# Two plain weight pairs instead of one at the head of each down unit, and the working pools moved to the other end of on-chip memory, in a two-layer decoder trunk on one core

## The chip, the core and the metric

The kernel runs on one core of a Trainium2 chip. The core has a matrix engine (TensorE, "PE" in the profile, with its weight loads as "PEld"), a vector engine (VectorE, "DVE"), a scalar engine (ScalarE, "ACT"), GpSimd ("POOL") and SyncE ("SP"), which issues the DMA transfers. Each engine works through its own list of instructions in order; the engines wait for each other through semaphores. Operands lie in the on-chip memory SBUF; matmul results are summed in PSUM, which has eight banks of 128 x 512 fp32 numbers. The metric is the time of one execution on the device in microseconds (us).

## What is computed

The reference is two layers over 256 tokens of width 2048, all in fp32. Each layer projects the normalised input, runs two groups of attention heads (gated linear attention and stick-breaking attention), projects their outputs back and adds them; then comes the part that the change touches:

```python
hm = rms_norm(x, mlp_norm)
up = jnp.square(jax.nn.relu(jnp.einsum('bsd,df->bsf', hm, w_up)))   # f = 8192
return x + jnp.einsum('bsf,fd->bsd', up, w_down)
```

## The kernel before

**How fp32 is multiplied.** Each fp32 operand is split into a high part in a format that the matrix engine takes whole, and a low part that is the rest. One product is then three matmuls: high by high, high by low, low by high. Weights are split when they arrive: ACT copies the raw tile to `whi`, DVE subtracts to get `wlo` (L358 and L360 in the other stages, `parts`, L987 to L992, in the down stage). There are four `whi` and four `wlo` buffers.

**Stages of the MLP.** The hidden width of 8192 is worked off in four quarters `q`. For each quarter, `mlp_up` computes eight pairs `i` of 256 hidden columns (L424 and L428 are its matmuls), applies the norm factor, the ReLU and the square, and splits the result into its parts (`up_forms`, L941). Then `mlp_down(q)` multiplies that quarter by its 2048 rows of `w_down`. With two layers there are eight such down stages.

**The down stage.** It has two units, `n2` = 0 and 1, of 1024 output columns each. A unit sums over eight pairs `j` of 128-row blocks. All its sums stay in eight PSUM banks, `m1` to `m8`, until the unit ends. There are two kinds of pair:

- A plain pair has two items, `left` (banks m2 and m4) and `right` (m3 and m8). Each item needs one `parts` call of 1024 elements per partition, and issues 12 matmuls.
- A fast pair multiplies 2 x 2 blocks with seven products instead of eight. It has four items with 6, 3, 6 and 6 matmuls; the third uses banks m5 and m7, the fourth m1 and m6. DVE first forms sums of weight blocks (L1042 to L1046), and `up_forms` has made sums of the activation blocks (tile `sx`, L945 to L952). `fast(i)` (L955) says which pairs are fast, for `up_forms` and for the down stage alike: 1, 3 and 5.

When the last fast pair of a unit has run (`lastf`, L1035), `drain` (L1049) adds banks 5, 1, 6 and 7 into the residual tiles `xb`: one ACT copy and eight DVE operations. After the `left` item of pair 7 `drain_left` adds banks 2 and 4 (two DVE operations), and after its `right` item `drain_right` adds banks 3 and 8. In the last stage each of these adds is followed by a store of the output (L1029). The next unit takes the same eight banks again, so its first matmul into a bank waits until that bank has been added.

**What sets the order.** Within the down stage the order on PE, DVE and ACT is written out by hand (`manual_schedule`, L1129). A list `queue` keeps items prepared ahead (`LEAD` = 4, L1098): item i+3 is prepared, then item i is multiplied, then whatever follows item i (a drain) is issued. So on DVE a drain stands behind the preparation of the item three places on, and everything that is prepared later stands behind the drain. At the edges of the stage a scheduler mixes the neighbouring stage's instructions in. The order is fixed when the program is built.

**Loads.** `load(x)` (L970) fetches pair x of the stage, 1 MB, four pairs ahead. Two of five go to buffers in the stage's own pool (`raw2`), three of five to buffers in the weight pool (`raw`).

**Where PSUM goes next.** After the down stage the eight banks become two accumulators of two banks (banks of m5, m1 and of m6, m7) and four single-bank tiles `ps`. After layer 0's last down stage the second layer begins with transposes of `xb` into `ps` tiles (`norm_operand`, L294); the first of these tiles has the bank of m2 and the second that of m8.

**Pools.** SBUF pools are stacked from the low end: constants, residual tiles, activations (`act`), weights (raw, whi, wlo), temporaries, small statistics, and on top the pool of the current stage, which is opened and closed by `open_scope` (attention tiles, or for the MLP `sx`, `ts`, `t4` and `raw2`).

Of the kernel before, what the change touches and what calls it, by code (L numbers as in the profile page):

```python
# [39 lines left out]
def trunk_kernel(  # L40
# [26 lines left out]
    cpool = ctx.enter_context(tc.tile_pool(name="const", bufs=1))  # L67
    xpool = ctx.enter_context(tc.tile_pool(name="resid", bufs=1))
    apool = ctx.enter_context(tc.tile_pool(name="acts", bufs=19))
    wpool = ctx.enter_context(tc.tile_pool(name="weights", bufs=3))  # L70
    tpool = ctx.enter_context(tc.tile_pool(name="temps", bufs=2))
    spool = ctx.enter_context(tc.tile_pool(name="stats", bufs=6))

    pools = {}
    scopes = {}
# [28 lines left out]
    def tmp(tag, shape, dt=F32, bufs=2):  # L104
        pool = pools["att"] if tag in ATT else pools["mlp"] if tag in MLP else tpool
        return pool.tile(list(shape), dt, tag=tag, name=nm(tag), bufs=bufs)
# [497 lines left out]
    for l in range(DEPTH):  # L604
# [336 lines left out]
        def up_forms(op, i, t):  # L941


            if fast(i):
                a11, a21, a12, a22 = (t[:, k, r * P : (r + 1) * P] for k in range(2) for r in range(2))  # L945
                e = tmp("t2", [P, 3, P], bufs=4)
                d = op.x[i] = tmp("sx", [P, 3, 2, P], F32R, bufs=3)
                nc.vector.tensor_tensor(e[:, 2, :], a21, a11, ALU.subtract)
                nc.vector.tensor_tensor(a21, a21, a22, ALU.subtract)
                nc.vector.tensor_tensor(e[:, 0, :], a11, a21, ALU.subtract)  # L950
                nc.vector.tensor_tensor(e[:, 1, :], a12, e[:, 0, :], ALU.subtract)
                split(d, e)  # L952
            split(op.pair(i), t)

        def fast(i):  # L955
            return i in (1, 3, 5)

        hT = Operand()
        ssq2 = new_ssq()
# [1 line left out]
        def mlp_down(q):  # L961
# [25 lines left out]
            def parts(r, n=2):  # L987
                hi = wpool.tile([P, 2, 512], F32R, tag="whi", name=nm("whi"), bufs=4)
                lo = wpool.tile([P, 2, 512], F32R, tag="wlo", name=nm("wlo"), bufs=4)
                nc.scalar.activation(hi[:, :n], r, AF.Copy)  # L990
                nc.vector.tensor_tensor(lo[:, :n], r, f32(hi[:, :n]), ALU.subtract)  # L991
                return hi, lo  # L992

            def mm(m, a, w, c, last):

                (ah, al), (wh, wl) = a, w
                o = banks[m]
                nc.tensor.matmul(o, ah, wh[:, c], start=m not in begun, stop=False)
                begun.add(m)
                nc.tensor.matmul(o, ah, wl[:, c], start=False, stop=False)  # L1000
                nc.tensor.matmul(o, al, wh[:, c], start=False, stop=last)

            def add(dst, a, b, sub=False):
                nc.vector.tensor_tensor(dst, a, b, ALU.subtract if sub else ALU.add)  # L1004
# [6 lines left out]
            def steps(x):  # L1011

                n2, j = pairs[x]
                last = j == 7
                r = raws[x]
                d = op.t[j]
                x11, x21, x12, x22 = (xb[2 * n2 + c][:, tt, :] for c in range(2) for tt in range(2))

                def blk(k, tt):
                    sl = slice(tt * P, (tt + 1) * P)  # L1020
                    return d[:, k, 0, sl], d[:, k, 1, sl]

                def ext(i):
                    return op.x[j][:, i, 0, :], op.x[j][:, i, 1, :]

                def store(c, tt):
                    if end:
                        n = 2 * n2 + c
                        nc.sync.dma_start(  # L1029
                            ov[:, tt, n * 512 : (n + 1) * 512], xb[n][:, tt, :]  # L1030
                        )

                if fast(j):
                    sums = {}
                    lastf = j == 5  # L1035

                    def first():
                        t13 = sums["t13"] = tmp("ts", [P, 2, 512], bufs=2)
                        t4 = sums["t4"] = tmp("t4", [P, 512], bufs=1)
                        b12 = r[:, 0, 512:]  # L1040
                        ends = r.rearrange("p k (c n) -> p (k c) n", c=2)[:, ::3, :]
                        nc.vector.tensor_tensor(  # L1042
                            t13, ends, b12.unsqueeze(1).to_broadcast([P, 2, 512]), ALU.add
                        )
                        add(b12, t13[:, 0, :], r[:, 1, 512:])
                        add(t4, b12, r[:, 1, :512])  # L1046
                        return parts(r[:, 1, :].rearrange("p (c n) -> p c n", c=2))

                    def drain():  # L1049
                        dw = tmp("t2", [P, 512], bufs=4)  # L1050
                        nc.scalar.activation(dw, banks[1], AF.Copy)
                        add(x12, banks[5], x12)
                        add(x22, banks[5], x22)
                        add(x11, banks[1], x11)
                        add(dw, banks[6], dw, True)
                        add(x12, dw, x12)
                        add(dw, banks[7], dw)
                        add(x21, x21, dw, True)
                        add(x22, dw, x22)

                    return (
                        (first, lambda w: (mm(2, blk(1, 0), w, 0, False), mm(3, ext(1), w, 1, False)), None),
                        (lambda: parts(sums["t4"].unsqueeze(1), 1), lambda w: mm(4, blk(1, 1), w, 0, False), None),
                        (lambda: parts(sums["t13"]),
                         lambda w: (mm(5, blk(0, 1), w, 0, lastf), mm(7, ext(2), w, 1, lastf)), None),
                        (lambda: parts(r[:, 0, :].rearrange("p (c n) -> p c n", c=2)),
                         lambda w: (mm(1, blk(0, 0), w, 0, lastf), mm(6, ext(0), w, 1, lastf)),
                         drain if lastf else None),
                    )

                def left(w):
                    for m, tt in ((2, 0), (4, 1)):
                        for k in range(2):
                            mm(m, blk(k, tt), w, k, last and k == 1)

                def right(w):
                    for m, tt in ((3, 0), (8, 1)):
                        for k in range(2):
                            mm(m, blk(k, tt), w, k, last and k == 1)

                def drain_left():
                    add(x11, banks[2], x11)
                    store(0, 0)
                    add(x21, banks[4], x21)
                    store(0, 1)

                def drain_right():
                    add(x12, banks[3], x12)
                    store(1, 0)
                    add(x22, banks[8], x22)  # L1090
                    store(1, 1)

                return (
                    (lambda: parts(r[:, :, :512]), left, drain_left if last else None),
                    (lambda: parts(r[:, :, 512:]), right, drain_right if last else None),
                )
# [13 lines left out]
            for x in range(len(pairs)):  # L1110
                load(x + 4)
                for prepare, products, follow in steps(x):
                    queue.append((x, products, prepare(), follow))
                    if len(queue) >= LEAD:
                        emit(*queue.pop(0))
# [25 lines left out]
def build(shapes):  # L1141
    import concourse.bacc as _bacc
    import numpy as _np
    from concourse import mybir as _mybir

    nc = _bacc.Bacc("TRN2", target_bir_lowering=False, num_devices=1)
    args = []
    for name in _INS:
        shape, dtype = shapes[name]
        args.append(  # L1150
            nc.dram_tensor(
                f"in_{name}_dram", shape, _mybir.dt.from_np(dtype), kind="ExternalInput"
            ).ap()
        )
    for i, (shape, dtype) in enumerate(_OUTS):
        dt = _mybir.dt.from_np(_np.dtype(dtype))
        args.append(nc.dram_tensor(f"out_{i}_dram", shape, dt, kind="ExternalOutput").ap())
    with tile.TileContext(nc) as tc:
        trunk_kernel(tc, *args)
    return nc  # L1160
# [10 lines left out]
```

## Time and profile before

| | |
|---|---|
| three runs | 2243.92, 2244.15, 2244.21 us, median 2244.15 us |
| profiled execution | 2244.34 us, its span 2242.6 us |
| granted TensorE clock | 1.000 over the span |
| PE busy | 2219.7 us, 99% of the span |
| DVE busy | 1628.6 us, 73% |
| ACT busy | 1171.0 us, 52% |
| DMA | 409.05 MB, mean 182 GB/s |

Times in the profile count from the start of the span. A row of the timeline gives the start, the duration, the engine, the source line, the operation, output tile `<-` input tiles, sizes and the number of merged instructions; in brackets stand the idle time before it and what ended that. Buffer numbers are left out of most tile names, but the banks show as `m__860` and the like: each unit numbers its banks anew, in the order m5, m1, m6, m7, m2, m4, m3, m8. Matmuls overlap in the pipeline: the next starts some 0.23 us after the one before, though each is shown with a duration near 0.39 us. So rates are read from starts. DVE operations too start up to 0.09 us before the one before has ended.

### The profile page before, as it was taken

How to read it: one execution, taken by the hardware profiler on the slowest of the kernel's cores; microseconds unless marked ns; L12 is line 12 of the kernel's file. 1: busy time of each engine (PE TensorE's matmuls, PEld its weight loads, DVE VectorE, ACT ScalarE, POOL GpSimd, SP SyncE). 2: the span in 40 equal slices, each digit the busy share in tenths (PEclk: the TensorE clock that was granted, in tenths of full speed). 3: DMA queues.
4: the chain of work that ended last, by engine and by line, in shares of the span. 5: the costliest groups of instructions: out<-in, count | busy, mean ns of one | idle time of the engine just before them, and what ended most of it. 6: DMA issues, size and time to landing. Idle time of an engine off the chain costs nothing.

```text
span 2242.6 us, 28461 instructions
## 1 busy us (share of the span) xinstructions
PE 2219.7 (99%) x11292; PEld 1858.6 (83%) x11292; DVE 1628.6 (73%) x2024; ACT 1171.0 (52%) x1499; POOL 39.1 (2%) x68
## 2 busy tenths in 40 slices
PE   9999999999999999999999999999999999999998
PEld 7988778887888888788788887888878878887887
DVE  5777565668868868867967775656787688688688
ACT  5555354555555455455555553555555545554553
POOL 0020000000000000000000200000000000000000
PEclk9999999999999999999999999999999999999999
DMA  6545446664665665565446544466656656656653
GB/s 228 189 158 162 151 144 232 187 188 169 214 186 188 201 188 187 190 195 179 169 135 204 171 151 150 154 225 184 188 183 203 187 178 207 188 181 210 185 180 127
DMA packets 250857, 409.05 MB, mean 182 GB/s; under 512 B 6650, under 2 KB 162882, under 8 KB 250724
## 3 DMA queue, kind: packets, MB, share of 16 engines
q1 hardware_dynamic: 250724, 407.24, 55.7%
q8 instruction: 88, 1.44, 0.3%
q14 instruction: 45, 0.37, 0.0%
HBM read 405.12 MB, written 2.10 MB: 182 GB/s over the span
## 4 chain that ended last, share of the span: by engine, by line
PE 91%; DVE 7%; issue 1%; ACT 1%; DMA 0%; POOL 0%; SPq 0%; POOLq 0%
PE acc L424 24%; PE acc L428 12%; PE acc L377 9%; PE acc L378 9%; PE acc L379 9%; DVE wlo L991 3%; DVE xb L1004 2%; DVE t L1004 1%; PE ps L294 1%; PE ps L847 1%; PE ps L859 1%; DVE ts L1042 0%; PE ps L806 0%; ACT whi L990 0%; PE ps L540 0%
## 5 line engine op out<-in xcount | busy, mean ns | idle before, releaser
L360 DVE TENSOR_TENSOR wlo<-raw,whi 128x1024 fp32r<-128x1024 f32 (+2 forms) x530 | 630.5, 1194 | 420.0 <-ACT whi L358 418.9
L358 ACT ACTIVATE whi<-raw 128x1024 fp32r<-128x1024 f32 (+2 forms) x530 | 545.3, 1032 | 643.9 <-PE acc L424 340.0
L424 PE MATMUL acc<-act,whi 128*128 128x512 f32 x2304 | 816.0, 399 | 0.0
L428 PE MATMUL acc<-act,wlo 128*128 128x256 f32 x2304 | 646.8, 281 | 0.0
L424 PEld LDWEIGHTS acc<-act,whi 128*128 128x128 f32 x2304 | 433.0, 188 | 106.5
L428 PEld LDWEIGHTS acc<-act,wlo 128*128 128x128 f32 x2304 | 435.2, 189 | 0.4
L377 PE MATMUL acc<-whi,act 128*128 128x512 f32 (+2 forms) x960 | 368.4, 384 | 0.5 <-ACT act L302 0.5
L378 PE MATMUL acc<-wlo,act 128*128 128x512 f32 (+2 forms) x960 | 361.9, 377 | 0.4 <-DVE wlo L360 0.4
L379 PE MATMUL acc<-whi,act 128*128 128x512 f32 (+2 forms) x960 | 361.6, 377 | 0.0
L991 DVE TENSOR_TENSOR wlo<-raw,whi 128x1024 fp32r<-128x1024 f32 x256 | 306.2, 1222 | 70.0 <-ACT whi L990 65.6
L990 ACT ACTIVATE whi<-raw 128x1024 fp32r<-128x1024 f32 x256 | 266.2, 1058 | 157.3 <-PE acc L424 29.0
L377 PEld LDWEIGHTS acc<-whi,act 128*128 128x128 f32 x960 | 180.9, 188 | 35.5 <-issue 4.1
L379 PEld LDWEIGHTS acc<-whi,act 128*128 128x128 f32 x960 | 180.5, 188 | 33.8 <-issue 0.7
L378 PEld LDWEIGHTS acc<-wlo,act 128*128 128x128 f32 x960 | 180.8, 188 | 32.0 <-DVE wlo L360 1.0
L990 ACT ACTIVATE whi<-t 128x512 fp32r<-128x512 f32 x48 | 30.4, 634 | 145.5 <-DVE t L1004 93.3
L991 DVE TENSOR_TENSOR wlo<-ts,whi 128x1024 fp32r<-128x1024 f32 x48 | 58.8, 1225 | 2.3 <-ACT whi L990 2.3
L1042 DVE TENSOR_TENSOR ts<-raw 128x1024 f32<-128x1024 f32 x48 | 58.5, 1218 | 0.0
L939 DVE TENSOR_TENSOR act<-t,act 128x512 fp32r<-128x512 f32 x64 | 44.1, 690 | 10.9 <-ACT act L938 10.9
L990 ACT ACTIVATE whi<-ts 128x1024 fp32r<-128x1024 f32 x48 | 50.2, 1045 | 0.0
L439 DVE TENSOR_TENSOR t<-acc,t 128x512 f32<-128x512 f32 x72 | 49.3, 684 | 0.0
L934 ACT ACTIVATE t<-t 128x512 f32<-128x512 f32 x64 | 39.6, 618 | 12.8 <-DVE t L930 12.8
L930 DVE SCALAR_TENSOR_TENSOR t<-t,row 128x512 f32<-128x512 f32 x64 | 44.3, 692 | 2.2
(1160 smaller groups left out, 2768.2 us busy)
## 6 DMA issues: line engine op xcount, KB each, us to landing
raw<-in_w_down_dram SPq DMA_DIRECT2D x128, 1024.0 KB, 5.3
raw<-in_w_up_dram SPq DMA_DIRECT2D x128, 1024.0 KB, 5.8
raw<-in_w_in_dram SPq DMA_DIRECT2D x84, 1024.0 KB, 5.1
raw<-in_w_o_dram SPq DMA_DIRECT2D x32, 1024.0 KB, 5.0
raw<-in_w_in_dram SPq DMA_DIRECT2D x14, 512.0 KB, 6.8
raw<-in_w_in_dram SPq DMA_DIRECT2D x8, 544.0 KB, 3.7
out_dram<-xb SPq DMA_DIRECT2D x8, 256.0 KB, 2.2
xb<-in_x_dram SPq DMA_DIRECT2D x3, 512.0 KB, 7.5
```

Of the source, the lines that this page charges most:

```text
L358: newest["hi"] = nc.scalar.activation(h, r, AF.Copy).ins
L360: newest["lo"] = nc.vector.tensor_tensor(lo[:, q : q + step, :width], r, f32(h), ALU.subtract).ins
L377: nc.tensor.matmul(o, xh[:, sl], whi[:, j, :width], start=first, stop=False)
L378: nc.tensor.matmul(o, xh[:, sl], wlo[:, j, :width], start=False, stop=False)
L379: st["mm"] = nc.tensor.matmul(o, xl[:, sl], whi[:, j, :width], start=False, stop=last).ins
L424: nc.tensor.matmul(acc[:, f, :], whi[:, j, sl], op.both(k), start=(k == 0), stop=False, skip_group_check=True,)
L428: nc.tensor.matmul(acc[:, f, T:], wlo[:, j, sl], xh, start=False, stop=(k == KT - 1), skip_group_check=True,)
L439: nc.vector.tensor_tensor(t, acc[:, :, :T], t, ALU.add)
L990: nc.scalar.activation(hi[:, :n], r, AF.Copy)
L991: nc.vector.tensor_tensor(lo[:, :n], r, f32(hi[:, :n]), ALU.subtract)
L1004: nc.vector.tensor_tensor(dst, a, b, ALU.subtract if sub else ALU.add)
L1042: nc.vector.tensor_tensor(t13, ends, b12.unsqueeze(1).to_broadcast([P, 2, 512]), ALU.add)
```

## The change

Fast pairs are now 2, 4 and 6 instead of 1, 3 and 5, so that a unit runs plain, plain, fast, plain, fast, plain, fast, plain. `lastf` follows, so `drain` is issued after pair 6 and one plain pair, not two, follows it in the unit. The number of matmuls, of splits and of loads is the same. Besides, the pools of weights, temporaries and statistics are allocated from the high end of SBUF, so that the stage's own pool now begins where the activations end.

```diff
-    wpool = ctx.enter_context(tc.tile_pool(name="weights", bufs=3))
-    tpool = ctx.enter_context(tc.tile_pool(name="temps", bufs=2))
-    spool = ctx.enter_context(tc.tile_pool(name="stats", bufs=6))
+    wpool = ctx.enter_context(tc.tile_pool(name="weights", bufs=3, side="right"))
+    tpool = ctx.enter_context(tc.tile_pool(name="temps", bufs=2, side="right"))
+    spool = ctx.enter_context(tc.tile_pool(name="stats", bufs=6, side="right"))
...
         def fast(i):
-            return i in (1, 3, 5)
+            return i in (2, 4, 6)
...
                 if fast(j):
                     sums = {}
-                    lastf = j == 5
+                    lastf = j == 6
```

## The prediction

> **What bounds the kernel now.** I read the page first, then the waits of PE, then the timeline around the one wait that repeats.
>
> ```profile
> span 2242.6 us, 28461 instructions
> PE 2219.7 (99%) x11292; PEld 1858.6 (83%) x11292; DVE 1628.6 (73%) x2024; ACT 1171.0 (52%) x1499; POOL 39.1 (2%) x68
> ...
> PE 91%; DVE 7%; issue 1%; ACT 1%; DMA 0%; POOL 0%; SPq 0%; POOLq 0%
> PE acc L424 24%; PE acc L428 12%; PE acc L377 9%; PE acc L378 9%; PE acc L379 9%; DVE wlo L991 3%; DVE xb L1004 2%; DVE t L1004 1%; PE ps L294 1%; PE ps L847 1%; PE ps L859 1%; DVE ts L1042 0%; PE ps L806 0%; ACT whi L990 0%; PE ps L540 0%
> ```
>
> PE is the bound. The change leaves its matmuls alone, so time can only come from or go into PE's waits:
>
> ```profile
> PE m__862_4746 L998 <- DVE xb L1004: 1.8, 1, 1.8
> ...
> PE m__3241_18213 L998 <- DVE xb L1004: 1.8, 1, 1.8
> PE ps L327 <- POOL ident masks.py:199: 1.5, 1, 1.5
> PE ps L294 <- DVE xb L1004: 1.1, 1, 1.1
> ```
>
> The first row stands eight times, once for each down stage: between its two units PE waits for a drain. The last row is the change of layers. The first of these places, on PE and then on DVE:
>
> ```profile
> 539.11 0.39 PE L1000 MATMUL m__791_4418<-wlo,sx 128*128 128x512 f32 x1
> 539.34 0.40 PE L1001 MATMUL m__791_4418<-whi,sx 128*128 128x512 f32 x1
> 539.58 0.40 PE L998 MATMUL m__793_4420<-whi,act 128*128 128x512 f32 x1
> ...
> 545.05 0.39 PE L998 MATMUL m__793_4420<-whi,act 128*128 128x512 f32 x1
> ...
> 550.49 0.39 PE L998 MATMUL m__860_4744<-whi,act 128*128 128x512 f32 x1
> ...
> 552.98 0.39 PE L1001 MATMUL m__861_4745<-whi,act 128*128 128x512 f32 x1
> 555.13 0.47 PE L998 MATMUL m__862_4746<-whi,act 128*128 128x512 f32 x1 [1.76 <-DVE xb L1004]
> 555.44 0.39 PE L1000 MATMUL m__862_4746<-wlo,act 128*128 128x512 f32 x1
> 555.67 0.39 PE L1001 MATMUL m__862_4746<-whi,act 128*128 128x512 f32 x1
> ```
>
> ```profile
> 536.05 4.83 DVE L991 TENSOR_TENSOR wlo<-raw,whi 128x1024 fp32r<-128x1024 f32 x4 [1.11 <-ACT whi L990]
> 540.80 1.28 DVE L1004 TENSOR_TENSOR xb<-m__789_4416,xb 128x512 f32<-128x512 f32 x2
> ...
> 545.38 0.68 DVE L1004 TENSOR_TENSOR xb<-t,xb 128x512 f32<-128x512 f32 x1
> 545.98 3.49 DVE L991 TENSOR_TENSOR wlo<-raw,whi 128x1024 fp32r<-128x1024 f32 x3
> 549.38 0.68 DVE L1004 TENSOR_TENSOR xb<-m__793_4420,xb 128x512 f32<-128x512 f32 x1
> 549.98 0.68 DVE L1004 TENSOR_TENSOR xb<-m__794_4421,xb 128x512 f32<-128x512 f32 x1
> 550.58 1.22 DVE L1042 TENSOR_TENSOR ts<-raw 128x1024 f32<-128x1024 f32 x1
> ...
> 554.30 0.68 DVE L1004 TENSOR_TENSOR xb<-m__795_4422,xb 128x512 f32<-128x512 f32 x1
> ```
>
> Call T the moment when the last fast pair is through and the next plain pair starts: 539.58. PE does pair 6 (to 545.05), pair 7 (to 550.49), then `left` of the next unit. A plain pair lasts 545.05 - 539.58 = 5.47 us, a half 2.73. DVE from T: the last split ahead of the drain, the drain (540.80 to 545.98, 5.18 us), three splits (to 549.38), bank 2 and 4, the sums and split of the next fast pair (550.58 to 554.30, 3.72 us), bank 3. Bank 2 is added at 549.38 + 0.68 = 550.06, 0.43 us before PE wants it: no wait. Bank 3 is added at 554.98, PE restarts 0.15 later: 555.13 - 552.98 = 2.15 us between two starts instead of 0.23, a loss of 1.92 us. Eight stages: 15.4 us.
>
> **The change, part by part.** *Between units.* The next unit now begins with two plain pairs, so the 3.72 us of sums leave the gap between bank 4 and bank 3: that wait goes. What is late next is bank 2. After the drain PE has one plain pair left, so it wants bank 2 at T + 5.47, not T + 10.91. DVE is as far as before at T, since what goes ahead of the drain is the same: the split three items on, whose ACT copy waits for a buffer that the item before the last releases, in both orders six matmuls (1.4 us) before T. So
>
> - drain starts T + 1.22 (540.80 - 539.58), ends T + 6.40;
> - one split instead of three stands before bank 2 (the second one, by `LEAD`, comes after): (549.38 - 545.98) / 3 = 1.13, T + 7.53;
> - bank 2 added: + 0.68, T + 8.21; PE restarts + 0.15, T + 8.36.
>
> PE loses 8.36 - 5.47 = 2.89 us. Then bank 4 (0.60 after bank 2, wanted 1.36 after), one split, bank 3 at T + 10.6 against T + 11.1: no second wait. Net 2.89 - 1.92 = +0.97 a stage, times 8 = **+7.8 us**. Bounds: the restart took 0.05 to 0.15 us in the rows here and below, and the drain's start can shift by a split (1.13): a wait of 1.7 to 3.1 us, -1.8 to +9.4 us over eight. I take the chain as it stands, since each of its rows keeps its place in the order.
>
> *Change of layers.* Before, DVE was through with `drain` long before the stage ended.
>
> ```profile
> 1121.50 1.22 DVE L360 TENSOR_TENSOR wlo<-raw,whi 128x1024 fp32r<-128x1024 f32 x1
> 1122.63 0.69 DVE L1004 TENSOR_TENSOR xb<-m__1603_9039,xb 128x512 f32<-128x512 f32 x1
> 1123.23 1.22 DVE L360 TENSOR_TENSOR wlo<-raw,whi 128x1024 fp32r<-128x1024 f32 x1
> 1124.37 0.69 DVE L1004 TENSOR_TENSOR xb<-m__1604_9040,xb 128x512 f32<-128x512 f32 x1
> ```
>
> ```profile
> 1123.42 0.60 PE L294 MATMUL ps<-ident,xb 128*128 128x128 f32 x4
> 1125.11 1.53 PE L294 MATMUL ps<-ident,xb 128*128 128x128 f32 x12 [1.09 <-DVE xb L1004]
> ```
>
> Four transposes into the bank of m2 start as the stage ends; the next twelve wait for bank 8 and start 1.69 us after the stage's end. In the changed program's order, DVE has after T: banks 5, 5, 1, 6 of the drain; a split of the next stage; one add; a split; bank 7; a split; two adds; then banks 2, 4, 3, 8. An add takes 0.60 from start to start (1122.63 to 1123.23), a split 1.13. The drain starts 0.19 after T (a row below: an add starts 0.42 after the last matmul's start, here T - 0.23). Eleven adds before bank 8 at 0.60, three splits at 1.13, bank 8 0.69: 0.19 + 6.60 + 3.39 + 0.69 = T + 10.87, PE + 0.05. The stage ends at T + 5.47, so the twelve transposes start 5.45 us after it, not 1.69: **+3.8 us**, once. Lower bound 0.4 (no split in between: 3.39 less), upper 5 (one more split).
>
> *The other six stage ends* go to an up stage with the same DVE list. Its first three splits end at T + 3.8, 5.5 and 7.3, the fourth at T + 12.0. PE wants them at T + 5.47 and every 2.8 us after (24% + 12% of 2242.6 us over 2304 pairs of matmuls is 0.35 us, eight to a tile): the fourth at T + 13.9. Cover 1.7 us at the least. I cost this at nothing; if the cover fails, each us is 6 us.
>
> *The end of the kernel.*
>
> ```profile
> 2238.71 0.69 DVE L1004 TENSOR_TENSOR xb<-m__3242_18214,xb 128x512 f32<-128x512 f32 x1 [0.67 <-PE m__3242_18214 L1001]
> ```
>
> ```profile
> 2238.29 0.39 PE L1001 MATMUL m__3242_18214<-whi,act 128*128 128x512 f32 x1
> ```
>
> Before, the last add ends 1.11 us after the last matmul's start, T + 5.47 - 0.23 + 1.11 = T + 6.35 by the new T. After, drain and four adds: 0.19 + 5.18 + 3 x 0.60 + 0.69 = T + 7.86. That is +1.5 us. The four stores of the output now start 0.6 us apart instead of up to 1.4:
>
> ```profile
> DMA to landing us min/median/max: 2.1/2.2/4.2
> ```
>
> Some of them may share the way; I add 0.2 (0 to 2.0, the maximum less the median). **+1.7 us.**
>
> *Head of the stage and moved sums.* The extra activation sums (L948 to L952) move from pairs 1, 3, 5 to 2, 4, 6, so one set falls on the change from up to down. There the down stage now prepares two plain pairs, and 3.72 us of weight sums and three further splits move out of that place. Nothing PE waits for gets later. The DMA queue keeps its order and its five buffers; a load lands 5.3 us after its issue and is issued four pairs ahead, some 20 us: nothing.
>
> ```profile
> raw<-in_w_down_dram SPq DMA_DIRECT2D x128, 1024.0 KB, 5.3
> ```
>
> *The pools.*
>
> ```profile
> L991 DVE TENSOR_TENSOR wlo<-raw,whi x256: 1216/1222/1228, 501.2 to 2234.0; 128x1024 fp32r<-128x1024 f32 x128
> L998 PE MATMUL m__795_4422<-whi,sx x3: 404/404/404, 514.7 to 535.4; 128*128 128x512 f32 x3
> ```
>
> Splits that read raw from the stage's pool (7 of 16) and from the weight pool differ by 1% at most between the extremes: place does not show on DVE. Matmuls with `sx` are closer to slow: 404 ns against 390 to 400 with `act`, and they start 0.235 apart, not 0.227. If that came from place, the 432 with `sx` could gain 0.008 us each, -3.5 us, or the 2928 matmuls of the down stages (16 units of 183) lose as much each, +23 us. I take 0: the first row is about place alone, the second also about where in the sequence.
>
> Sum: 7.8 + 3.8 + 1.7 = +13.3 us. The profiled execution took 2244.34 us, so 2257.6; the median of the runs is 0.19 lower: **2257.5 us**.
>
> **The rivals.**
>
> *A. As summed*, 2254 to 2261 us.
>
> *B. Only the wait between units grows*, the ends being hidden by work that I count as later: 2244.15 + 7.8 = 2252. The chain of adds at the layer's change, fixed in order, speaks against it.
>
> *C. Faster: bank 2 comes in time.* Then the eight waits go with the sums that caused them and nothing takes their place: -15.4, and with the two ends 2244.15 - 15.4 + 5.5 = 2234. Its place is DVE between T and T + 5.47: it decides at a chain 2.89 us shorter. The split before the drain (1.22) and the one before bank 2 (1.13) together give 2.35, so even without both bank 2 is late. Against it.
>
> *D. The long gaps cost the clock.*
>
> ```profile
> 6.25 1.48 PE L327 MATMUL ps<-ident 128*128 128x128 f32 x6
> ...
> 9.23 0.62 PE L379 MATMUL acc<-whi,act 128*128 128x512 f32 x1
> 9.65 0.43 PE L377 MATMUL acc<-whi,act 128*128 128x512 f32 x1
> ```
>
> At the kernel's start matmuls stand 0.42 us apart, against 0.227 later, until 9.65; counted from 6.25 that is 3.4 us at about half speed, 1.7 us lost. If each of the nine longer gaps did this: 9 x 1.7 = 15 more, 2273. After today's gaps of 1.9 us the next starts are 0.31 and 0.23 apart: no slowing.
> [...]
>
> *E. The place of the pools tells on the matmuls*, by up to 0.008 us on the 2928: 23 us either way, 2234 to 2281. For it speaks the `sx` row, against it the even splits.
>
> **How the numbers follow.** Under 0.2% (4.5 us) two versions of this kernel can hardly be told apart. A 0.78, B 0.08, C 0.04, D 0.03, E 0.07. Faster: C and a quarter of E, 0.06. Same: a quarter of E, and B with its waits at their lower bound, 0.04. Slower: the rest, 0.90. The time is that of A; the range 2250 to 2263 holds A and B with the bounds of the unknown terms.
>
> **What would show it.** In the waits of PE, eight rows of about 2.7 us on the first matmul of a unit's bank 2 (`left`), none on bank 3; at the change of layers L294 waits of together about 4.8 us; PE busy as before. An up stage that waits for L360 right after a down stage, or L998 groups with another mean, would make me wrong.

## The result and the profile after

The changed kernel took 2279.47 us (median of four runs, 2277.18 to 2288.14), the kernel before 2244.18 us beside it: a ratio of 1.0164, 95% interval 1.0138 to 1.0191. The forecast was 2257.5 us with a range of 2250 to 2263. The direction was right, but the slowdown is 35 us where I had reckoned 13. The profiled execution of the changed kernel took 2280.27 us; its span is 2278.6 us, 36.0 us more than before, and its mean granted clock 0.996.

The waits of PE, in the columns "total us, times, longest us":

```profile
PE ps L294 <- DVE xb L1004: 4.3, 2, 3.2
PE m__1105_6170 L998 <- DVE xb L1004: 2.6, 1, 2.6
...
PE m__2496_13909 L998 <- DVE xb L1004: 2.6, 1, 2.6
```

There are eight rows like the last two, and all are on the first matmul of bank 2 of a new unit. None is on bank 3 any more. The first such place, on PE and then on DVE (start, duration):

```profile
558.48 0.40 PE L1001 MATMUL m__794_4418<-whi,act 128*128 128x512 f32 x1
561.45 0.47 PE L998 MATMUL m__858_4739<-whi,act 128*128 128x512 f32 x1 [2.58 <-DVE xb L1004]
```

```profile
554.32 1.28 DVE L1004 TENSOR_TENSOR xb<-m__787_4411,xb 128x512 f32<-128x512 f32 x2
...
559.49 1.22 DVE L991 TENSOR_TENSOR wlo<-raw,whi 128x1024 fp32r<-128x1024 f32 x1
560.62 0.68 DVE L1004 TENSOR_TENSOR xb<-m__791_4415,xb 128x512 f32<-128x512 f32 x1
```

The drain starts at 554.32, one split follows it at 559.49, and bank 2 is added from 560.62 to 561.30. PE restarts 0.15 us later: 561.45 - 558.48 = 2.97 us between two starts instead of 0.23, a loss of 2.74 us. Before it was 1.92. Eight times 0.82 is 6.6 us.

The change of layers, on PE:

```profile
1139.38 0.40 PE L1001 MATMUL m__1602_9035<-whi,act 128*128 128x512 f32 x1
1143.03 0.76 PE L294 MATMUL ps<-ident,xb 128*128 128x128 f32 x4 [3.25 <-DVE xb L1004]
1144.82 1.54 PE L294 MATMUL ps<-ident,xb 128*128 128x128 f32 x6 [1.03 <-DVE xb L1004]
```

The stage ends at 1139.61 and the transposes that need bank 8 start 5.21 us later, against 1.69 before: +3.5 us. The end of the kernel:

```profile
2272.63 0.39 PE L1001 MATMUL m__3240_18209<-whi,act 128*128 128x512 f32 x1
...
2274.30 0.68 DVE L1004 TENSOR_TENSOR xb<-m__3240_18209,xb 128x512 f32<-128x512 f32 x1
```

From the last matmul's start to the end of the span are 2278.6 - 2272.63 = 5.97 us; before, 2242.6 - 2238.29 = 4.31: +1.7 us. These three come to 11.8 us. The other 24 of the 36 are in no wait of PE and not in the tail.

**The matmuls themselves have another pace.** I cut both traces at the same instructions: 95 matmuls of a projection (L377 to L379), the second up stage (256 pairs of L424 and L428), and the first 180 matmuls of the first down stage. The view of windows gives the window, its length, PE's busy time and count, the granted clock, and the DMA share and rate. (Counts at the edges differ by one or two, since neighbours overlap.) Before:

```profile
352.70:374.25 21.55, 21.55 (x97) 1.00 0.58 200
594.41:684.86 90.45, 90.45 (x514) 1.00 0.64 198
508.54:549.81 41.27, 41.27 (x183) 1.00 0.50 172
```

After:

```profile
358.35:380.51 22.16, 22.16 (x96) 1.00 0.55 190
604.22:692.97 88.75, 88.75 (x513) 1.00 0.63 196
516.01:558.01 42.00, 42.00 (x182) 1.00 0.53 187
```

No wait lies in these windows and the clock is full in all of them. Still the projection goes from 0.227 to 0.233 us per matmul, the down stage from 0.229 to 0.233, and the up stage gets 1.7 us shorter. Over all starts in the two traces the 512-column matmuls of the projections average 233.0 ns instead of 227.6 (2496 of them: +13.5 us), those of the down stages 233.3 instead of 229.2 (2928: +12.0), and five of the eight up stages are 1.7 us shorter (-8.5). That is +17.0 us.

**And the clock falls at three places.** One of them, in windows of 3.41 us:

```profile
907.97:911.38 3.41, 3.41 (x16) 1.00 1.01 383
911.38:914.80 3.42, 1.42 (x7) 0.99 0.17 68
914.80:918.21 3.41, 2.82 (x7) 0.50 0.71 210
918.21:921.62 3.41, 3.41 (x10) 0.51 0.49 167
921.62:925.04 3.42, 3.42 (x17) 1.00 0.61 237
```

In the second window PE waits for bank 2. In the third and the fourth the granted clock is half, and only 10 matmuls go through the fourth, where 17 go through the fifth: some 1.6 us lost. The trace has five such windows, in stretches of 6.83, 6.83 and 3.41 us at a granted clock of 0.50 that begin at 914.8, 1143.4 and 2051.4 us, each near the end of a wait. The starts inside them come 6.0 us later than at the ordinary pace. What is left of the 36.0 us after 11.8 and 17.0 is 7.2, which fits.

So the working theory was: the waits are as forecast, the place of the pools costs 17 us on the matmuls, and the longer waits cost 6 to 7 us of clock.

### The profile page after: what moved, and what is told of

Same layout as the page of the kernel before. It is cut to its first block, busy times and chain, and to the rows that moved or that the text cites. A ratio compares the mean times of both kernels' runs of the same rounds, so it can differ in the third digit from the quotient of the medians.

```text
span 2278.6 us, 28474 instructions
## 1 busy us (share of the span) xinstructions
PE 2244.5 (99%) x11292; PEld 1861.2 (82%) x11292; DVE 1625.3 (71%) x2024; ACT 1172.4 (51%) x1499; POOL 39.1 (2%) x68
## 4 chain that ended last, share of the span: by engine, by line
PE 93%; DVE 4%; issue 1%; ACT 1%; DMA 0%; POOL 0%; SPq 0%; DVEq 0%; POOLq 0%
PE acc L424 23%; PE acc L428 12%; PE acc L377 9%; PE acc L378 9%; PE acc L379 9%; DVE xb L1004 2%; DVE wlo L991 1%; PE ps L294 1%; DVE t L1004 1%; PE ps L847 1%; PE ps L859 1%; ACT whi L990 0%; PE ps L806 0%; PE ps L540 0%; PE ps L486 0%
## 5 line engine op out<-in xcount | busy, mean ns | idle before, releaser
L424 PE MATMUL acc<-act,whi 128*128 128x512 f32 x2304 | 807.3, 395 | 0.0
L428 PE MATMUL acc<-act,wlo 128*128 128x256 f32 x2304 | 646.3, 281 | 0.0
L424 PEld LDWEIGHTS acc<-act,whi 128*128 128x128 f32 x2304 | 432.6, 188 | 99.8
L428 PEld LDWEIGHTS acc<-act,wlo 128*128 128x128 f32 x2304 | 433.8, 188 | 0.4
L991 DVE TENSOR_TENSOR wlo<-raw,whi 128x1024 fp32r<-128x1024 f32 x256 | 308.1, 1221 | 95.0 <-ACT whi L990 90.2
L377 PE MATMUL acc<-whi,act 128*128 128x512 f32 (+2 forms) x960 | 373.4, 389 | 0.8 <-ACT act L302 0.8
L378 PE MATMUL acc<-wlo,act 128*128 128x512 f32 (+2 forms) x960 | 367.4, 383 | 0.0
L379 PE MATMUL acc<-whi,act 128*128 128x512 f32 (+2 forms) x960 | 366.5, 382 | 0.0
L377 PEld LDWEIGHTS acc<-whi,act 128*128 128x128 f32 x960 | 181.3, 189 | 40.4 <-issue 4.1
L379 PEld LDWEIGHTS acc<-whi,act 128*128 128x128 f32 x960 | 180.9, 188 | 38.4 <-issue 0.7
L990 ACT ACTIVATE whi<-ts 128x1024 fp32r<-128x1024 f32 x48 | 50.5, 1052 | 21.6 <-PE m__1353_7602 L1001 2.2
```

Source lines behind the costliest of these rows:

```text
L377: nc.tensor.matmul(o, xh[:, sl], whi[:, j, :width], start=first, stop=False)
L378: nc.tensor.matmul(o, xh[:, sl], wlo[:, j, :width], start=False, stop=False)
L379: st["mm"] = nc.tensor.matmul(o, xl[:, sl], whi[:, j, :width], start=False, stop=last).ins
L424: nc.tensor.matmul(acc[:, f, :], whi[:, j, sl], op.both(k), start=(k == 0), stop=False, skip_group_check=True,)
L428: nc.tensor.matmul(acc[:, f, T:], wlo[:, j, sl], xh, start=False, stop=(k == KT - 1), skip_group_check=True,)
```

## The experiments

**Each half alone.** First the pools alone, with the pairs of before:

```diff
-    wpool = ctx.enter_context(tc.tile_pool(name="weights", bufs=3))
+    wpool = ctx.enter_context(tc.tile_pool(name="weights", bufs=3, side="right"))
     (tpool and spool likewise)
```

> The pools move, the pairs stay 1, 3, 5. Theory P (the place of the weight pools sets the spacing of the matmuls): the eight waits between units stay at 1.92 us, the clock stays at 1.000, and the spacing is that of the changed kernel: down stages 233 ns, input and output projections 233 ns, up stages 231 and 118 ns. Against before that is 2930 x 4.1 + 2500 x 5.4 - 2304 x 3.8 ns = 12 + 13.5 - 9 = +17 us: 2261 us. Rival O (the spacing comes from the order of the pairs): 2244 us, spacing 229, 228 and 236 ns.

Measured: 2259.04 us, ratio 1.0063 (1.0048 to 1.0078), clock 1.000. The projection and the up stage in the same windows:

```profile
357.02:379.19 22.17, 22.17 (x97) 1.00 0.57 190
601.69:690.44 88.75, 88.75 (x514) 1.00 0.65 200
```

The matmuls have the pace of the changed kernel. The eight waits did not stay at 1.92 us as expected but fell to 1.54, since the slower matmuls cover more of the chain of adds; that makes 3 us less. The pools alone carry the slower pace, without any loss of clock. Then the pairs alone:

```diff
-            return i in (1, 3, 5)
+            return i in (2, 4, 6)
...
-                    lastf = j == 5
+                    lastf = j == 6
```

> The pairs become 2, 4, 6, the pools stay. Theory P: the waits of the changed kernel (eight of 2.6 to 2.9 us on bank 2, some 4.5 us at the change of layers), spacing as before (229, 228, 236 ns), so +13 us from waits, and some of these gaps halve the clock for 3.4 or 6.8 us as they did in the changed kernel, 1.5 to 3.5 us each, 0 to 10 us in all: 2257 to 2267 us. Rival O: spacing 233 ns too, 2274 us and more.

Measured: 2266.64 us, ratio 1.0099 (1.0084 to 1.0114), clock 0.995.

```profile
352.64:374.19 21.55, 21.55 (x97) 1.00 0.60 199
```

The pace is that of before. The eight waits are there, each a loss of 2.89 us, and five stretches of half clock. So the pairs alone cost 22 us, more than my whole sum of 13.3, because of the clock.

**What about the pools' place is it?** In the kernel before all activation tiles and all weight buffers start on multiples of 64 bytes. In the changed one the weight buffers start 32 bytes past one (196576). The first test moves them back by 32 bytes at the high end of SBUF, the second shifts them by 32 bytes at the old end:

```diff
+    padpool = ctx.enter_context(tc.tile_pool(name="pad", bufs=1, side="right"))
+    padpool.tile([P, 8], F32, name="pad_t")
     wpool, tpool, spool with side="right"
```

> The pools move as in the changed kernel, but 32 bytes of padding at the end of SBUF put whi and wlo at addresses that 64 divides (196544 instead of 196576); pairs 1, 3, 5. Theory PA (it is the alignment to 64 bytes): spacing as before, 2244 us. Theory PR (it is the region, the far end of SBUF): spacing 233, 233 and 231 ns, 2261 us.

```profile
352.59:374.17 21.58, 21.58 (x97) 1.00 0.59 197
593.63:684.07 90.44, 90.44 (x513) 1.00 0.64 198
508.45:549.31 40.86, 40.86 (x182) 1.00 0.51 173
```

Measured: 2248.19 us, ratio 1.0015 (1.0006 to 1.0025). The same three windows have the pace of before, and the down stage is faster than ever: 40.86 us for 180 matmuls against 41.27. So it is not the end of SBUF. The 4 us that remain are clock (0.996): the waits are 2.02 us here, and five stretches of 3.41 us are at half speed. They cost some 7.7 us by the starts inside them, more than is left, since the down stages are faster.

```diff
+    padpool = ctx.enter_context(tc.tile_pool(name="pad", bufs=1))
+    padpool.tile([P, 8], F32, name="pad_t")
     wpool = ctx.enter_context(tc.tile_pool(name="weights", bufs=3))
```

> The pools stay where they were, moved by 32 bytes (whi from 140992 to 141024); pairs 1, 3, 5. Theory PA: spacing 233, 233 and 231 ns, 2261 us. Theory PR: spacing as before, 2244 us.

Measured: 2262.96 us, ratio 1.0087 (1.0070 to 1.0104), with the slow pace (22.15 us for the projection and 42.01 us for the down stage). 32 bytes at the old end do the same harm. The gain of the up stage is not as steady: three of the eight up stages have it here, five with the pools alone.

**Whose place?** Next the activations are shifted by 32 bytes, once alone and once with everything behind them:

```diff
+    padpool = ctx.enter_context(tc.tile_pool(name="pad", bufs=1))
+    padpool.tile([P, 8], F32, name="pad_t")
     apool = ctx.enter_context(tc.tile_pool(name="acts", bufs=19))
+    pad2 = ctx.enter_context(tc.tile_pool(name="pad2", bufs=1))      # the first kernel alone
+    pad2.tile([P, 8], F32, name="pad2_t")
     wpool = ctx.enter_context(tc.tile_pool(name="weights", bufs=3))
```

> The kernel before, with 32 bytes put ahead of the pool of activations and 32 more behind it: the activations now start 32 bytes past a multiple of 64 (38624), the weight buffers and the sums sx stay on one. Three theories. Only the weight buffers' place counts: nothing changes, spacing 0.236 us in the up stage, 0.228 in the projections, 2244 us. The difference of the two counts: as in the kernels with shifted weights, 0.231 and 0.233, about 2259 us. The role counts (an operand that streams through is slow at 32, one that is loaded as stationary is faster there; activations stream in the up stage and are stationary elsewhere): up stage 0.241, projections and down stage 0.222, about 2230 us.

> The kernel before, with 32 bytes put ahead of the activations alone, so that activations, weight buffers and all that follows start 32 bytes past a multiple of 64. Only the weight buffers' place counts: spacing 0.231 us in the up stage, 0.233 elsewhere, 2259 to 2261 us. The difference counts: nothing changes, 2244. The role counts: the two shifts cancel, up 0.236, elsewhere 0.228, 2244.

Activations alone: 2267.25 us, ratio 1.0094 (1.0079 to 1.0109).

```profile
358.19:380.36 22.17, 22.17 (x96) 1.00 0.55 191
602.88:693.32 90.44, 90.44 (x514) 1.00 0.64 197
```

Everything: 2245.07 us, ratio 1.0000 (0.9991 to 1.0010).

```profile
354.08:375.67 21.59, 21.59 (x97) 1.00 0.56 198
596.00:686.44 90.44, 90.44 (x514) 1.00 0.65 198
510.05:551.35 41.30, 41.30 (x182) 1.00 0.50 173
```

In these runs the difference between the two places decides, not either place: shifting one operand by 32 bytes costs (2262.96 us with the weights, 2267.25 with the activations), shifting both is free (2245.07). The theories of the weights' place and of the roles fall. Counted modulo 256, the distance from activations to weights is 32 bytes with the activations alone shifted, just as in the changed kernel and in the runs with the pools alone and with the weights shifted at the old end. The projections and the down stages have the same slow pace in all four: 22.15 to 22.17 us and 41.99 to 42.01 us in these windows. But of the eight up stages none gained in the profiled execution here, where five, five and three gained in those; that is why the time is 2267 and not the 2259 expected. The four runs of this kernel lie between 2261.58 and 2267.80 us, so the number of stages that gain may differ from execution to execution; only one of them was profiled.

A clash with other work is not the cause either. In the changed kernel 76 gaps between starts (23 in the down stages, 53 in the projections) fall where no instruction of ACT, DVE or GpSimd and no DMA packet was under way, and they average 0.234 us; 49 such gaps in the kernel before average 0.227.

**Waits and clock apart.** The changed kernel with its buffers mended (the high end and 32 bytes):

```diff
     the diff of the change, and
+    padpool = ctx.enter_context(tc.tile_pool(name="pad", bufs=1, side="right"))
+    padpool.tile([P, 8], F32, name="pad_t")
```

> The changed kernel (pairs 2, 4, 6, pools at the high end) with 32 bytes more at that end, so that the weight buffers start on multiples of 64 bytes. If the place of the weight buffers modulo 64 is all that the pools did, this is the pairs' change alone: the kernel with pairs 1, 3, 5 and the same pools had a span of 2244.7 us, of which about 7.6 went to half clock, so 2237.1 at full clock; eight waits of 2.90 instead of 2.02 us (+7.0), the change of layers (+3.7), the end (+1.7): 2249.5, and 5 to 9 stretches of half clock at 1.7 us or more each: 2258 to 2265 us, matmuls of the down stage 0.227 us apart. If pairs and pools act on each other beyond that, the time stays near 2275.

Measured: 2268.71 us, ratio 1.0106 (1.0091 to 1.0121), clock 0.991. Each of the eight waits loses 3.0 us, and the pace is that of the mended pools. At full clock that makes 2250.3 us (the expectation had 2249.5, with waits of 2.9); the span is 2266.1, so the clock cost 16 us, more than I had allowed for: eight of the nine waits are followed by half clock, three times for two windows, eleven windows in all. Next the wait is taken away instead, in the kernel with the pairs alone, by holding back the drain between the units:

```diff
+            held = []
...
-                         drain if lastf else None),
+                         held.append(drain) if lastf and n2 == 0 and not end else drain if lastf else None),
...
                 def drain_right():
                     add(x12, banks[3], x12)
                     store(1, 0)
                     add(x22, banks[8], x22)
                     store(1, 1)
+                    if held:
+                        held.pop()()
```

> Pairs 2, 4, 6 with the pools as before, and in seven of the eight down stages the drain after the first unit is held back behind the adds of banks 2, 4, 3 and 8. If the wait on bank 2 is the drain's place in DVE's order, seven waits go and nothing takes their place: 2244.2 - 7 x 1.92 + 1.0 (the eighth stage) + 3.7 + 1.7 = 2237 us; if the half clock comes from these waits, only the change of layers and the eighth stage are left for it, 1.7 us each: 2239 to 2241. If the half clock comes from the order of the pairs whatever the waits, the five stretches of the kernel with pairs 2, 4, 6 stay: 2246 or more. If the held drain makes the weight splits late, new waits on L991 take the place: 2244 to 2250.

Measured: 2240.74 us, ratio 0.9983 (0.9974 to 0.9992), with the pairs 2, 4, 6 and the old pools. The two largest waits of PE that remain:

```profile
PE ps L294 <- DVE xb L1005: 4.5, 2, 3.4
PE m__3237_18206 L999 <- DVE xb L1005: 2.7, 1, 2.7
```

Seven of eight waits are gone, nothing takes their place, and the clock falls after these two alone: 0.998 over the span, against 0.995 with all the waits and the same pairs. So the half clock comes from the waits and not from the order of the pairs. With the mended pools as well:

> As the kernel with the held drain, and with the pools at the high end and 32 bytes more there (weight buffers on multiples of 64). The same as that kernel less 2928 matmuls x 0.0022 us (down stage 0.227 apart instead of 0.229) = 6.4 us: 2231 to 2235 us. If that gain of spacing belonged to the pairs 1, 3, 5 only: 2239.

Measured: 2234.35 us, ratio 0.9954 (0.9938 to 0.9971). That is 6.4 us less than with the held drain alone. The gain in the down stage belongs to the pools' place and adds to the other.

**How long must a wait be?** The kernel before keeps all as it is, and one DVE operation makes its waits a little longer:

```diff
                         add(x22, dw, x22)
+                        if n2 == 0:
+                            add(dw[:, :256], dw[:, :256], dw[:, :256])
```

> The kernel before, with one more DVE operation of 256 columns (its result is not used) at the end of the drain between the units: the eight waits of 1.92 us become about 2.2, all else stays. If idle time of more than about 2 us inside one stretch of 3.4 us sets the clock to half for the next stretch, +2 us for the waits and 1.7 us for each of 4 to 8 stretches: 2253 to 2260 us, with granted clock under 1. [...]

Measured: 2253.28 us, ratio 1.0038 (1.0023 to 1.0053), clock 0.998. The wait is 2.1 us at all eight places. Three of them are followed by half clock; these stretches start at 909.9, 1852.0 and 2207.0 us. I cut the trace from the first of these starts in steps as long as the shortest half-clock stretch of the changed kernel (3.41 us, from 2051.4 us on). For four of the waits, two with half clock behind them and two without, the rows are the window that holds most of the wait and the window behind.

```profile
729.01:732.43 3.42, 1.91 (x9) 1.00 0.90 361
732.43:735.84 3.41, 2.99 (x13) 1.00 0.00 0
906.49:909.91 3.42, 1.50 (x7) 1.00 0.72 281
909.91:913.32 3.41, 3.41 (x9) 0.50 0.00 0
1671.09:1674.51 3.42, 1.61 (x8) 1.00 0.86 347
1674.51:1677.92 3.41, 3.30 (x15) 1.00 0.04 11
1848.62:1852.03 3.41, 1.46 (x7) 0.99 0.61 243
1852.03:1855.44 3.41, 3.41 (x10) 0.51 0.02 5
```

Where PE was busy for 1.50 or 1.46 us of a window, the next one ran at a clock of 0.50 or 0.51. At 1.61 and 1.91 it did not: there part of the same wait lies in the next window, in which PE was busy for 3.30 and 2.99 us. My estimate from these four pairs is that the idle time inside one window counts, and not the length of the wait; no run shows what sets the windows. Over the runs, the eight waits of 1.54 us (the pools alone) and of 1.92 us (before) left the clock at 1.000. With 2.02 us (the pools mended by 32 bytes) five stretches were at half clock and the mean was 0.996; with 2.1 us here three, and 0.998; with 2.89 us (the pairs alone) five, and 0.995.

**Can the up stage have the gain alone?** It gains where the others lose, so its weights alone are put 32, or 16, bytes on:

```diff
+    def part_tile(tag, n, off=0):
+        t = wpool.tile([P, 1040], F32R, tag=tag, name=nm(tag), bufs=4)
+        return t[:, off : off + 1024].rearrange("p (k n) -> p k n", n=n)
...                                   (whi and wlo come from it everywhere)
-            for s, (whi, wlo) in enumerate(weight_parts(w2d, 8 * g * P, c0, 8, 256)):
+            for s, (whi, wlo) in enumerate(weight_parts(w2d, 8 * g * P, c0, 8, 256, off=8)):
```

> The kernel with pairs 2, 4, 6, held drain and mended pools, and in the up stage alone the split weights lie 32 bytes past a multiple of 64 (the buffers are 64 bytes longer and the up stage's view of them starts 8 numbers in). If the difference between the two operands' places decides for each matmul by itself, the up stage alone goes to 0.231 and 0.118 us (2304 x -0.0048 + 2304 x 0.001 = -8.8 us), projections and down stage stay at 0.228 and 0.227: 2225 to 2226 us. If the spacing hangs on where the whole pool lies and not on the two addresses that a matmul reads, the up stage stays at 0.236 and 0.117: 2234 us.

> The same with 16 bytes in place of 32. If only the half of 64 bytes in which the operands lie counts, 16 bytes change nothing, up stage 0.236, 2234 us; if any difference from a multiple of 64 does it, 0.231, 2226 us.

Measured: 2246.24 us (ratio 1.0005, 0.9996 to 1.0014) with 32 bytes and 2246.96 us (1.0009, 1.0000 to 1.0018) with 16. Neither theory had this. The windows with 32 bytes:

```profile
355.46:377.42 21.96, 21.96 (x97) 1.00 0.57 193
596.29:685.72 89.43, 89.43 (x513) 1.00 0.64 195
511.62:553.26 41.64, 41.64 (x183) 1.00 0.54 189
```

The up stage gained 1.0 us of 90.4, but the projection and the down stage became slower (21.96 and 41.64 us, against 21.58 and 40.86 with the mended pools), though all their buffers lie on multiples of 64. With 4160 bytes to a buffer only one in four of them lies a multiple of 256 bytes from the activations. My reading "modulo 64" was wrong. The next runs try other distances:

```diff
-        t = wpool.tile([P, 1040], F32R, tag=tag, name=nm(tag), bufs=4)
+        t = wpool.tile([P, 1088], F32R, tag=tag, name=nm(tag), bufs=4)
```

> As the run with the up stage's weights 32 bytes on, but the weight buffers are 4352 bytes long, 17 times 256, instead of 4160, 65 times 64. In that run the down stage had become slower (0.231 us) though every buffer lay on a multiple of 64. If the difference of the two operands' places counts modulo 256, the down stage is back at 0.227 and the projections at 0.228, while the up stage keeps 0.231 to 0.232: 2234.4 - 2304 x (0.0044 - 0.0008) = 2226 us. If it was the view into longer buffers that cost, whatever their length: 2246 us again.

```diff
     the kernel before, and
+    padpool = ctx.enter_context(tc.tile_pool(name="pad", bufs=1))
+    padpool.tile([P, 32], F32, name="pad_t")
     wpool = ctx.enter_context(tc.tile_pool(name="weights", bufs=3))
```

> The kernel before, with 128 bytes put between the activations and the weight buffers. If the difference counts modulo 64 or 128, nothing changes: 2244 us. If it counts modulo 256, the projections and the plain pairs go from 0.228 to about 0.235 us (the spacing that the kernel before shows where sx lies 128 bytes off): 4847 matmuls x 0.0075 = +36 us, less up to 11 in the up stage: 2269 to 2281 us. The sums sx move along with the weight buffers and stay at their 0.235.

With buffers of 17 x 256 bytes: 2234.94 us, ratio 0.9956 (0.9941 to 0.9971).

```profile
354.27:375.85 21.58, 21.58 (x97) 1.00 0.59 197
593.22:683.66 90.44, 90.44 (x513) 1.00 0.64 194
510.15:550.96 40.81, 40.81 (x183) 1.00 0.54 191
```

With 128 bytes between activations and weights: 2258.70 us, ratio 1.0062 (1.0045 to 1.0079).

```profile
357.72:379.80 22.08, 22.08 (x96) 1.00 0.58 195
601.32:691.20 89.88, 89.88 (x513) 1.00 0.64 198
514.60:556.43 41.83, 41.83 (x183) 1.00 0.50 173
```

The first of these was to come to 2226 us. Projection and down stage are back at 21.58 and 40.81 us in the first and slow in the second, at 22.08 and 41.83, so lying a multiple of 64 or of 128 bytes apart was not enough. The size in the second was less than I took from the `sx` rows: 0.2325 us, not 0.235. Nor did the sums `sx`, still 128 bytes off, stay at 0.235: they too went to 0.2324. In the kernel before, where only they are off, the matmuls with `sx` come in threes, with 0.238 us from the first start to the second and 0.232 from the second to the third. My estimate from these spacings is that 0.235 holds a cost of changing the distance and that 0.2325 is the pace of a distance that is kept; no run shows the two apart. A difference of 256 modulo 512 (the mended pools) was as fast as one of 0 (21.58 us for the projection against 21.59 with everything shifted), so multiples of 256 bytes had the fast pace in all these runs. But the up stage did not gain with 32 bytes this time, and those are the 8 us that are missing. The last run puts its weights 96 bytes on (`off=24`):

> As the run with longer buffers, with 96 bytes for the up stage instead of 32. If any difference that is no multiple of 256 speeds the up stage alike, 2226 us as with 32; if each has its own spacing, the up stage goes to 0.228 to 0.230 as it did in the run with 4160 bytes where the difference came out at 160 modulo 256: 2234.4 - 2304 x (0.007 - 0.001) = 2220 us.

```profile
352.31:373.89 21.58, 21.58 (x97) 1.00 0.58 198
589.73:678.48 88.75, 88.75 (x514) 1.00 0.63 196
506.62:547.47 40.85, 40.85 (x183) 1.00 0.56 191
```

Measured: 2220.57 us, ratio 0.9893 (0.9878 to 0.9907). All three kinds of stage now have, within 0.04 us, the shortest times that were seen in these windows. This version has the pairs 2, 4, 6, the held drain, the pools at the high end, weight buffers at 256-byte distances from the activations, and the up stage's weights 96 bytes off. It beats the changed kernel by 59 us and the kernel before by 24.

## Why the prediction was wrong, point by point

- **What bounds the kernel: half right.** PE is the bound, and 11.8 of the 36 us are longer waits of PE and the longer tail behind its last matmul. That "time can only come from or go into PE's waits" because the change leaves the matmuls alone was wrong: 17 us came from matmuls that were the same in number and shape but slower, and some 7 from the clock.
- **Between units: right.** Forecast: no wait on bank 3, the drain at T + 1.22, bank 2 added at T + 8.21, a loss of 2.89 us. Measured: T is 24 slower matmuls (5.6 us) before 558.72, that is 553.1, so the drain came at T + 1.2, the add ended at T + 8.2, and PE lost 2.74 us. The difference of 0.15 is the slower pace itself: the plain pair, which covers part of the chain, takes 5.6 us and not 5.47. In the run with the pairs alone, at the pace of before, the loss is the forecast 2.89 us.
- **Change of layers and end: right.** +3.8 forecast, +3.5 measured; +1.7 forecast, +1.7 measured. Of the last, the exact match is luck: the adds took 1.2 us more, not 1.5, and the stores 0.4, not 0.2. The other stage ends and the head of the stage cost nothing, as taken: no row of PE's waits names the weight splits behind a down stage.
- **The pools: the step that failed.** The term of the sum at which I wrote "I take 0" measured +17.0 us. The sign was in the profile: the 432 matmuls with `sx` stood 0.235 us apart and not 0.227. I weighed that row against the even durations of DVE's splits, which stayed as they were when the matmuls slowed down (mean 1222 ns before, 1221 after), and put the rest down to the place in the sequence. The runs show it was place: `sx` lay 128 bytes off, modulo 256, from the weights, and where its distance became a multiple of 256 the down stage lost that time (41.27 to 40.86 us). My upper bound of +23 us left the 2496 projection matmuls out, and I had no row for the gain of the up stage. Rival E, with a chance of 0.07, had the pools' place as the cause. That the top of its span, 2281 us, lies near the measured time is luck: it holds 23 us for the down stages alone, where they lost 12, and nothing for the projections, the up stages and the clock.
- **Rival D: the second failure.** I gave it a chance of 0.03, since gaps of 1.9 us had left the pace alone. In the changed kernel two of the eight waits and the change of layers led to half clock; in the changed kernel with mended pools, with waits of 3.0 us, it was eight of nine. A window of half clock that PE filled cost 1.5 to 1.6 us (the runs with 2.02 and 2.1 us of wait), close to the 1.7 that I had priced; one with part of a wait in it cost less.

## What to carry to other kernels

When a change moves a pool, compare the distance between the two operands of the hot matmuls before and after, and read the pace from the starts of the same run of matmuls in both traces. In these runs 32 or 128 bytes past a multiple of 256 cost the projection 0.5 to 0.6 us of 21.6; the share of PE's busy time (99% before and after) and its waits don't show that. Count a stall of the matrix engine twice, once as the time lost and once as a possible stretch of half clock behind it: here waits of 1.92 us had none, and of the eight of 2.1 us three had one, which cost 1.5 to 1.6 us where PE filled it. And look whether a chain of adds that stands before those a new unit wants first can be issued behind them; with the pairs 2, 4, 6 that alone turned a loss of 22 us into a gain of 4.

## What was not expected of the hardware

- The pace of this kernel's matmuls, with the same shapes, changed with the distance between stationary and moving operand. Where activations are stationary and weights stream it was 0.227 us at a multiple of 256 bytes (21.55 to 21.59 us for the 95 matmuls of the projection) and 0.2325 to 0.233 us at 32 or 128 bytes (22.08 to 22.17). The up stage, where the roles are exchanged and every second matmul has 256 columns, was the other way round: 90.44 or 90.45 us for the second stage at a multiple of 256, 88.75 at its shortest (the changed kernel, the pools alone, and 96 bytes). Why is not shown.
- The up stage has two paces at one and the same distance. In the changed kernel three of the eight up stages are as slow as before and five are not, with the same buffers and a full clock; the second to fourth of them:

```profile
604.22:692.86 88.64, 88.64 (x256) 47.88 (x255) 1.00 0.63 196
781.19:869.82 88.63, 88.63 (x256) 47.88 (x255) 1.00 0.63 195
960.97:1051.29 90.32, 90.32 (x256) 47.86 (x255) 1.00 0.62 192
```

  This is the view of windows for L424 alone, with PE's and then the weight loads' busy time. At the same distance of 32 bytes modulo 256 none of the eight had the fast pace in the run with buffers of 17 x 256 and in the one with the activations alone shifted (90.44 us for the second); with 96 bytes all had it (88.75). What selects the pace is open.
- Equal waits had different prices in one execution: of the eight waits of 2.1 us of the matrix engine, three were followed by a stretch at half clock (for two of them the view has 3.41 us at 0.50 and 0.51) and five by none. What decides is not shown.
